# A diffusion block with a mixture of experts: gate/up of both experts of the first pair in turn, and router, heads, modulation steps, overflow branch and last pair rearranged

## The chip, the cores and the metric

The program runs on one core of one Trainium2 chip. The metric is the device time of one execution in microseconds (us). The names of the engines are those of the profile: PE is the matrix engine, PEld its weight loads, DVE the vector engine, ACT the scalar engine, POOL the general-purpose engine, SP the engine that issues the DMA transfers.

## The reference

256 latent tokens and 256 context tokens, 2048 wide, pass one block. Cut to what is computed:

```python
mod_x = jnp.split(jax.nn.silu(c) @ w_ada + b_ada, 6, axis=-1)          # 2048 x 12288
mod_c = jnp.split(jax.nn.silu(c_ctx)[None] @ w_ada + b_ada, 6, axis=-1)
qr, kr, vr, gr, cq, ckv, kpe = split_projection(modulate(x, mod_x[0], mod_x[1]) @ w_in)
qr_c, kr_c, vr_c, gr_c, cq_c, ckv_c, kpe_c = split_projection(modulate(ctx, mod_c[0], mod_c[1]) @ w_in)
...
o_ret = bidirectional_retention(qh, kh, to_heads(vr, 8), log_gamma, s_fwd, s_bwd)   # qh, kh: rope
ret = retention_output(o_ret, gr, ret_gn_w)
att = block_attention(q, concat(k_ctx, k_lat), concat(v_ctx, v_lat))    # 8 heads, low-rank q and kv
mix = jnp.concatenate([ret, from_heads(att)], -1) @ w_o
h = layer_norm(DEEPNORM_ALPHA * x + mod_x[2][:, None] * mix, ln1_w, ln1_b)
y = moe(modulate(h, mod_x[3], mod_x[4]))       # 4 groups of 8 experts, top group, top 2 in it
return layer_norm(DEEPNORM_ALPHA * h + mod_x[5][:, None] * y, ln2_w, ln2_b)
```

Each of the 32 experts has a gate and an up matrix of 2048 x 512 and a down matrix of 512 x 2048, in 4-byte numbers.

## The kernel before

A scheduler orders the instructions of each engine by the dependencies and the order of the source, so that the place in the source is only a wish, except in a block under `manual_schedule`, which keeps the source's order on the engines that it names. DMA loads are all issued by SP, in one order, each as soon as its buffer is free and SP has come to it.

**Input projection.** `w_in` is taken in six stages of 1, 1, 2, 4, 4 and 4 blocks of 128 rows (`STAGES`); within a stage ten blocks of columns pass, one load of 1 MB each in the stages of four (`win_chunks` gives their order, `ci` counts them). Each load is split into a high part (ACT, L273) and a low part (DVE, L274), and three matmuls for each 128x128 block multiply them (L594 to L596); a DVE addition collects the result (L603). Between the column blocks stand the pieces of the first two modulation vectors of the next stage: `piece(j, m)` loads 1 MB and issues matmuls with 32 rows of output (L526) for the shift (m=0) or the scale (m=1), into column groups 0, 1 or 2, 3 of the PE. All these loads turn over four buffers, `st`. `ada_steps` adds steps of the other four modulation vectors, 64 loads of 1 MB with two DVE multiply-adds each (L250); `ADA_V` says how many follow each column block, and at the end of the shift and scale for the experts `ada_finish` sums over the partitions with 16 one-column matmuls (L215).

**Heads.** In the last stage the rope on k (on POOL, L312 to L317) follows block ci=3; the rope on q (DVE), the decay tables and all eight retention heads (`ret_tables`, `ret_head`) follow ci=5, ahead of the last four blocks of columns. Latent attention and then the output projection `W_o` (L852 to L854, n = 0 to 3 for the column blocks) come after. With the first step of `W_o` four DVE reductions form the constants of the router (L810).

**Router.** After `W_o` the layer norm (L181, L182), the logits, the choice of the experts (L944 to L954) and the one-hot tables `oh` follow, mainly on DVE; PE waits for the choice at L957.

**Experts.** They go in 16 pairs (`pr`). A pair gathers its tokens with matmuls (`gather_two`, L1049, copied out by DVE L1058 and ACT L1055), multiplies them with gate and up (`gate_up`, L1071: expert e in four loads of 2 MB, c0 to c3), flips the hidden values, multiplies them with down (`down`, L1116, two loads d0 and d1; ACT L1122 and DVE L1123 split the result in a high and a low part) and puts it back (`scatter`, two matmuls L1130, DVE L1131 and L1132), which for most pairs stands in the next pair's `gate_up`. The loads (L1030) turn over six buffers, so that load n+6 waits until the matmuls of load n are done; the order of the loads is the list `order`. `overflow` after pair 5 is a branch for the case that more than 64 tokens chose one expert; it is not taken, but the branch is there. In the last pair (`final`) the two experts' down are interleaved, and statistics and the last norm follow.

## Time and profile before

| | us |
|---|---|
| median of three runs | 1685.78 |
| lowest and highest of them | 1684.48, 1687.98 |
| the profiled execution | 1686.18 |
| its span in the trace | 1684.4 |
| PE busy in it | 1521.6 |
| DVE busy in it | 919.9 |
| mean granted clock of the PE | 0.972 |

The span is the time from the first to the last record; what lies around it is 1.8 us here. A busy share alone says little: the stretches of the program have different limits, so that the rows further down are read stretch by stretch, for what each engine waits for.

### The profile page before, as it was taken

How to read it: one execution, taken by the hardware profiler on the slowest of the kernel's cores; microseconds unless marked ns; L12 is line 12 of the kernel's file. 1: busy time of each engine (PE TensorE's matmuls, PEld its weight loads, DVE VectorE, ACT ScalarE, POOL GpSimd, SP SyncE). 2: the span in 40 equal slices, each digit the busy share in tenths (PEclk: the TensorE clock that was granted, in tenths of full speed). 3: DMA queues.
4: the chain of work that ended last, by engine and by line, in shares of the span. 5: the costliest groups of instructions: out<-in, count | busy, mean ns of one | idle time of the engine just before them, and what ended most of it. 6: DMA issues, size and time to landing. Idle time of an engine off the chain costs nothing. (4 is left out here: it accounts for less than half of the span.)

```text
span 1684.4 us, 20454 instructions
## 1 busy us (share of the span) xinstructions
PE 1521.6 (90%) x8316; PEld 919.2 (55%) x8316; DVE 919.9 (55%) x1553; ACT 484.2 (29%) x913; POOL 105.9 (6%) x91
## 2 busy tenths in 40 slices
PE   5999999988889999699999988799989989899994
PEld 4667686877768767444543543444445345336432
DVE  6877584899698768824423532432342343234238
ACT  3323232324675534431320211121122013103112
POOL 1000000053513010000000000000000000000001
PEclk8999999998999999899999999999999999999997
DMA  8787777766554579579999999999999999999993
GB/s 326 272 326 283 294 309 286 276 245 225 184 192 153 199 270 360 225 301 426 426 427 427 426 427 425 370 428 427 427 427 427 427 426 427 426 426 427 421 425 136
DMA packets 54226, 579.28 MB, mean 344 GB/s; under 512 B 6320, under 2 KB 6768, under 8 KB 8816
## 3 DMA queue, kind: packets, MB, share of 16 engines
q1 hardware_dynamic: 54000, 577.90, 84.2%
q8 instruction: 67, 1.10, 0.3%
q14 instruction: 31, 0.25, 0.0%
q0 software_dynamic: 128, 0.03, 0.0%
HBM read 575.81 MB, written 2.10 MB: 343 GB/s over the span
## 5 line engine op out<-in xcount | busy, mean ns | idle before, releaser
L1071 PE MATMUL pA<-we,xg 128*64 128x512 f32 x2048 | 468.0, 602 | 12.8 <-DMA we<-in_wexp_dram 12.8
L1071 PEld LDWEIGHTS pA<-we,xg 128*64 128x64 f32 x2048 | 140.8, 138 | 281.2 <-issue 247.6
L1116 PE MATMUL pA<-we,hT 128*64 128x256 f32 x2048 | 232.7, 382 | 17.4 <-DMA we<-in_wexp_dram 16.1
L1123 DVE SCALAR_TENSOR_TENSOR D<-pA,gcol,D 64x256 fp32r<-64x256 f32 x256 | 123.5, 482 | 176.0 <-ACT D L1122 175.3
L273 ACT CAST whi<-st 128x1024 fp32r<-128x1024 f32 (+3 forms) x130 | 125.1, 965 | 282.5 <-PE pA L596 172.5
L1116 PEld LDWEIGHTS pA<-we,hT 128*64 128x64 f32 x2048 | 147.4, 137 | 92.2 <-ACT D L1122 8.7
L595 PE MATMUL pA<-wlo,xhi 128*128 128x512 f32 (+1 forms) x480 | 188.2, 392 | 10.5 <-DVE wlo L274 10.5
L594 PE MATMUL pA<-whi,xhi 128*128 128x512 f32 (+1 forms) x480 | 185.5, 394 | 3.3 <-ACT whi L273 3.1
L596 PE MATMUL pA<-whi,xlo 128*128 128x512 f32 (+1 forms) x480 | 185.8, 387 | 0.0
L250 DVE SCALAR_TENSOR_TENSOR ada_acc<-st,c,ada_acc 128x1024 f32<-128x1024 f32 x128 | 177.5, 1406 | 8.3 <-DMA st<-in_ada_dram 8.2
L274 DVE TENSOR_TENSOR wlo<-st,whi 128x1024 fp32r<-128x1024 f32 (+2 forms) x122 | 134.6, 1112 | 57.6 <-ACT whi L273 57.1
L1122 ACT ACTIVATE D<-pA,gcol 64x256 fp32r<-64x256 f32 x256 | 120.0, 469 | 156.7 <-PE pA L1116 87.5
L1074 ACT ACTIVATE hid<-pA 128x256 f32<-128x256 f32 x32 | 12.3, 383 | 493.5 <-PE pA L1071 493.5
L1075 DVE TENSOR_TENSOR hid<-pA,hid 128x256 f32<-128x256 f32 x32 | 13.5, 423 | 219.7 <-ACT hid L1074 219.7
L594 PEld LDWEIGHTS pA<-whi,xhi 128*128 128x128 f32 x480 | 90.5, 191 | 37.5 <-ACT whi L273 17.7
L595 PEld LDWEIGHTS pA<-wlo,xhi 128*128 128x128 f32 x480 | 91.9, 191 | 31.9 <-DVE wlo L274 14.5
L1058 DVE TENSOR_SCALAR xg<-pT,modt 128x256 f32<-128x256 f32 x64 | 34.8, 544 | 131.2 <-PE pA L1071 93.7
L1131 DVE TENSOR_TENSOR pA<-pA,ada_acc 128x512 f32<-128x512 f32 x128 | 83.5, 693 | 36.8 <-PE pA L1130 36.6
L596 PEld LDWEIGHTS pA<-whi,xlo 128*128 128x128 f32 x480 | 92.0, 192 | 16.3
L1049 PE MATMUL pT<-oh,nn 128*128 128x256 f32 x512 | 80.5, 303 | 9.1 <-DVEq L1136 5.8
L1049 PEld LDWEIGHTS pT<-oh,nn 128*128 128x128 f32 x512 | 68.3, 199 | 31.7 <-issue 20.5
L1132 DVE TENSOR_TENSOR h<-pA,h 128x512 f32<-128x512 f32 x128 | 82.6, 683 | 0.8
(353 smaller groups left out, 1578.6 us busy)
## 6 DMA issues: line engine op xcount, KB each, us to landing
we<-in_wexp_dram SPq DMA_DIRECT2D x190, 2048.0 KB, 21.8
st<-in_ada_dram SPq DMA_DIRECT2D x96, 1024.0 KB, 6.7
st<-in_win_dram SPq DMA_DIRECT2D x35, 1024.0 KB, 6.7
st<-in_wo_dram SPq DMA_DIRECT2D x16, 1024.0 KB, 4.9
we<-in_wexp_dram SPq DMA_DIRECT2D x4, 1024.0 KB, 17.4
st<-in_wuq_dram SPq DMA_DIRECT2D x3, 1024.0 KB, 4.8
xn<-in_x_dram SPq DMA_DIRECT2D x2, 1024.0 KB, 6.4
xn<-in_ctx_dram SPq DMA_DIRECT2D x2, 1024.0 KB, 17.0
```

What stands on the lines that cost most here:

```text
L250: V.scalar_tensor_tensor(accs[m][:, sl], w[:, sl], c2[:, k, 0:1], accs[m][:, sl], op0=OP.mult, op1=OP.add)
L273: A.copy(hi, src)
L274: (eng or V).tensor_tensor(lo, src, hi, op=OP.subtract)
L594: T.matmul(banks[t][:, :wd], xh[:, sl], hi[:, kk, :wd], start=fst, stop=False)
L595: T.matmul(banks[t][:, :wd], xh[:, sl], lo[:, kk, :wd], start=False, stop=False)
L596: T.matmul(banks[t][:, :wd], xl[:, sl], hi[:, kk, :wd], start=False, stop=lst)
L1049: T.matmul(p[:, 256 * j:256 * j + width], nnh[i % 2][:, i // 2, ks], oh[:, i // 2, :width], start=(i == 0), stop=(i == 3))
L1071: T.matmul(pg[64 * cg:64 * cg + 64], xg[:, k, c0:c0 + 64], c[:, kk, 512 * cg:512 * cg + 512], start=(k == 0), stop=(k == KB - 1))
L1116: T.matmul(pd[64 * cg:64 * cg + 64, :256], hT[:, f % 2, 64 * (f // 2):64 * (f // 2) + 64], c[:, f, 256 * cg:256 * cg + 256], start=(f == 0 ...
L1122: A.activation(hl[0][rows, sl], p, AF.Copy, scale=g)
L1123: V.scalar_tensor_tensor(hl[1][rows, sl], p, g, hl[0][rows, sl], op0=OP.mult, op1=OP.subtract)
L1131: V.tensor_tensor(p, p, mod5[:, sl], op=OP.mult)
```

## The change

- `piece(j)` takes both loads, shift and scale, and issues their matmuls in turn, so that four column groups of the PE follow each other; `GEMV_AT` places the pieces. The columns' order and `ADA_V` of the stages change; fewer `ada_steps` stand in the projection, more in the attention.
- `ada_finish` sums with four matmuls of 512 columns into the four column groups, an ACT copy and four transposes.
- The rope on k moves from POOL to DVE. Of the eight heads two follow each of ci=6 to 9, each head's tables two heads ahead.
- The four reductions of the router's constants are spread over four steps of `W_o`.
- Behind `W_o` the source's order is kept on DVE, ACT and PE. Only the norms that the first gathers need (c=0) and half of those of c=1 stand ahead of the choice of experts; the others follow it.
- In the first pair `gate_up` takes both experts, in turn for each gathered piece, and the first eight loads come in that order (`order[:8]`).
- The branch of `overflow` moves ahead of the downs of pair 5, whose gathers then run between the downs as in the other odd pairs.
- In the last pair D is kept whole (`new_D_whole`): no DVE subtraction, one matmul instead of two in `scatter`.

```diff
-ADA_V = [[0] * 10, [0] * 10, [0] * 5, [1] * 10, [1] * 10, [2] * 4 + [1] * 6]
+ADA_V = [[0] * 3, [1, 0, 0], [1, 1, 1, 0, 1], [1] * 7 + [0, 1, 1], [1] * 7 + [0, 1, 1], [1] * 10]
+
+GEMV_AT = (1, 3, 4, 5, 6)
...
+    elif si:
+        order = [0, 2, 1, 3, 6, 4, 7, 8, 5, 9]
...
-            for k in range(KB):
-                T.matmul(p[:, k:k + 1], acc[:, 128 * k:128 * k + 128], ones[:, 0:1], start=True, stop=True)
...
+            for g in range(4):
+                T.matmul(p[32 * g:32 * g + 32], ones[:, 0:32], acc[:, 512 * g:512 * g + 512], start=True, stop=True)
+            row = sa.tile([128, 2048], F32, name="st", tag="st")[:, :512]
+            A.copy(row, p)
+            p = bankT()
+            for j in range(4):
+                transpose(p[:, 128 * j:128 * j + 128], row[:, 128 * j:128 * j + 128])
...
-        def piece(j, m):
+        def piece(j):
...
+                c = [stream(dram2(a["ada01"], base + (m * nch + j) * 128 * per * w, 128, per * w), per * w)
+                     for m in range(2)]
                 for kk in range(per):
                     k = j * per + kk
-                    g = 2 * m + (k % 2)
-                    T.matmul(p[32 * g:32 * g + 32, :w], csil[:, k], c[:, kk * w:kk * w + w],
-                             start=(k < 2), stop=(k >= KB - 2))
+                    for m in range(2):
+                        g = 2 * m + (k % 2)
+                        T.matmul(p[32 * g:32 * g + 32, :w], csil[:, k], c[m][:, kk * w:kk * w + w],
+                                 start=(k < 2), stop=(k >= KB - 2))
...
-                            rope(pl["k"][:, t, 512 * j:512 * j + 512], t, "ck", "sk", 4, 64, R["rt"], G)
+                            rope(pl["k"][:, t, 512 * j:512 * j + 512], t, "ck", "sk", 4, 64, R["rt"])
...
-                    for h in range(H):
+                    for h in range(2):
                         ret_tables(h)
+                if ci > 5:
+                    for h in range(2 * ci - 12, 2 * ci - 10):
                         ret_head(h)
-                elif ci == LAT:
+                        if h < H - 2:
+                            ret_tables(h + 2)
+                if ci == LAT:
                     mla_latents()
...
+                if 1 <= 4 * n + k4 <= 4:
+                    router_const(4 * n + k4 - 1, rparts[4 * n + k4 - 1])
...
+        pinned = tc.manual_schedule(engines={V.engine, A.engine, T.engine})
+        pinned.__enter__()
...
+        norm_a(0, 0)
+        norm_a(1, 0)
+        V.reciprocal(hs[:, :, 1:2], hs[:, :, 1:2])
+        norm_b(0, 0)
+        norm_b(1, 0)
...
-    norms()
+    for c in range(1, 4):
+        for t in range(2):
+            if c > 1:
+                norm_a(t, c)
+            norm_b(t, c)
+            done, f = normed(t, c)
+            normed_lo(t, c, f)
...
+    order[:8] = [s * 6 + j for j in range(4) for s in range(2)]
...
-    def gate_up(xg, c0, src, before=None):
+    def gate_up(xg, experts, before=None):
...
+            for (c0, src), pg in zip(experts, pgs):
+                c = src(kc).rearrange("p (k n) -> p k n", k=2)
+                for kk in range(2):
+                    k = 2 * kc + kk
+                    for cg in range(2):
+                        T.matmul(pg[64 * cg:64 * cg + 64], xg[:, k, c0:c0 + 64], c[:, kk, 512 * cg:512 * cg + 512],
+                                 start=(k == 0), stop=(k == KB - 1))
...
+            if len(hl) > 1:
+                V.scalar_tensor_tensor(hl[1][rows, sl], p, g, hl[0][rows, sl], op0=OP.mult, op1=OP.subtract)
...
+            if len(hl) == 1:
+                T.matmul(p, sT[:K, t, :].bitcast(F32), hl[0][:K], start=True, stop=True)
...
+        pair = [(128 * pq + 64 * s, src[s]) for s in range(2)]
         if pr == 0:
-            router_weights()
-        hid1 = gate_up(xg, 128 * pq + 64, src[1], second)
+            hid0, hid1 = gate_up(xg, pair, first)
+            with tc.issue_after(done.ins):
+                router_weights()
+            for kc in range(8):
+                second(kc)
+        else:
+            hid0, = gate_up(xg, pair[:1], first)
+            hid1, = gate_up(xg, pair[1:], second)
         hT, sT, gcol = box["hT"], box["sT"], box["g"]
-        hl = new_D()
-        gather = pq and not final and pr != 5
+        if pr == 5:
+            overflow()
+        hl = new_D_whole() if final else new_D()
+        gather = pq and not final
```

The pieces of the modulation, on PE in the fourth stage. Before, the four matmuls of one piece stand between the triples of the projection:

```order
L594 MATMUL pA<-whi,xhi 128x512
L595 MATMUL pA<-wlo,xhi 128x512
L596 MATMUL pA<-whi,xlo 128x512
L526 MATMUL pG<-st,csil 32x512 x4
L594 MATMUL pA<-whi,xhi 128x512
L595 MATMUL pA<-wlo,xhi 128x512
```

The same place with the change (L603 to L605 are the projection's matmuls there, L535 the piece's):

```order
L603 MATMUL pA<-whi,xhi 128x512
L604 MATMUL pA<-wlo,xhi 128x512
L605 MATMUL pA<-whi,xlo 128x512
L535 MATMUL pG<-st,csil 32x512 x8
L603 MATMUL pA<-whi,xhi 128x512
L604 MATMUL pA<-wlo,xhi 128x512
```

Eight matmuls stand together where four stood; before, 13 such groups of four with 512 columns stood alone, and now none does, while in five of the 12 pieces with 512 columns one of the eight stands apart from the others.

The heads, on DVE in the last stage. Before, from the first head (`AM` are its scores, `stat` and `mv` its statistics) to the second:

```order
L396 TENSOR_TENSOR AM<-pA,Dt 128x256
L397 TENSOR_TENSOR AM<-pA,Dt 128x256
L250 SCALAR_TENSOR_TENSOR ada_acc<-st,c_71,ada_acc 128x1024 x2
L406 BN_STATS stat<-pA 128x6 x2
L407 BN_AGGR mv<-stat 128x2 x2
L396 TENSOR_TENSOR AM<-pA,Dt 128x256
```

With the change, from the first head to the second (L281 is the low part of a projection weight, L612 the projection's addition):

```order
L403 TENSOR_TENSOR AM<-pA,Dt 128x256
L404 TENSOR_TENSOR AM<-pA,Dt 128x256
L281 TENSOR_TENSOR wlo<-st,whi 128x1024
L612 TENSOR_TENSOR kvall<-pA,kvall 128x320 x4
L257 SCALAR_TENSOR_TENSOR ada_acc<-st,c_71,ada_acc 128x1024
L281 TENSOR_TENSOR wlo<-st,whi 128x1024
L413 BN_STATS stat<-pA 128x6 x2
L414 BN_AGGR mv<-stat 128x2
L257 SCALAR_TENSOR_TENSOR ada_acc<-st,c_71,ada_acc 128x1024
L414 BN_AGGR mv<-stat 128x2
L403 TENSOR_TENSOR AM<-pA,Dt 128x256
```

The column blocks that stood behind all eight heads now stand between them, with their splits and additions, and fewer halves of modulation steps do.

The first pair, on PE with the change, from the first `gate_up` on; between the rows shown are only gathers (`pA_5655` is the first expert's result with its loads c0 to c3 in `we_5642`, `we_5646`, `we_5650` and `we_5672`, `pA_5656` the second's in `we_5644`, `we_5648`, `we_5652` and `we_5708`):

```order
L1132 MATMUL pA_5655<-we_5642,xg_5654 64x512 x8
...
L1132 MATMUL pA_5655<-we_5646,xg_5654 64x512 x8
...
L1132 MATMUL pA_5655<-we_5650,xg_5654 64x512 x8
...
L1132 MATMUL pA_5656<-we_5644,xg_5654 64x512 x8
L1132 MATMUL pA_5656<-we_5648,xg_5654 64x512 x8
L1132 MATMUL pA_5656<-we_5652,xg_5654 64x512 x8
...
L1132 MATMUL pA_5655<-we_5672,xg_5654 64x512 x4
L1132 MATMUL pA_5656<-we_5708,xg_5654 64x512 x4
```

And the loads on SP with the change, from the first of the first pair on (`we_5672` takes the buffer of `we_5642`, `we_5708` that of `we_5644`, `we_5750` that of `we_5648`, `we_5714` that of `we_5646`):

```order
L1090 DMA we_5642<-in_wexp_dram 128x4096 [waits DMAHW5_49]
L1090 DMA we_5644<-in_wexp_dram 128x4096
L1090 DMA we_5646<-in_wexp_dram 128x4096 [waits DMAHW7_49]
L1090 DMA we_5648<-in_wexp_dram 128x4096 [waits DMAHW3_49,DMAHW2_49,DMAHW4_49,DMAHW1_49,DVE_49]
L1090 DMA we_5650<-in_wexp_dram 128x4096
L1090 DMA we_5652<-in_wexp_dram 128x4096
L1090 DMA we_5672<-in_wexp_dram 128x4096 [waits DMAHW5_49,PE_49]
L1090 DMA we_5708<-in_wexp_dram 128x4096 [waits DMAHW7_49,PE_49]
L1090 DMA we_5750<-in_wexp_dram 128x4096 [waits DMAHW1_49,PE_49]
L1090 DMA we_5714<-in_wexp_dram 128x4096 [waits DMAHW6_49,PE_49]
```

The second expert's pieces do not stand where the source has them: the first expert's first three go ahead, and c0 of the second stands behind c2 of the first, with six gathers between them. Before, the four pieces of the first expert came first and their loads stood first in the list.

## Rows read from the trace of the kernel before

**Rows 1.** Windows: start:end and length; busy PE, PEld, DVE, ACT, POOL; clock; DMA.

```profile
60.00:340.00 280.00, 278.69 (x1347) 199.53 (x1347) 199.04 (x255) 80.62 (x118) 2.30 (x2) 1.00 0.76 293
340.00:400.00 60.00, 54.17 (x221) 43.09 (x220) 56.46 (x75) 17.56 (x26) 30.34 (x28) 0.94 0.66 241
400.00:500.00 100.00, 83.50 (x451) 68.50 (x449) 84.95 (x176) 66.78 (x154) 39.47 (x32) 0.93 0.54 191
500.00:580.00 80.00, 75.19 (x443) 64.53 (x442) 67.92 (x120) 45.28 (x92) 15.23 (x6) 0.98 0.45 167
697.00:717.00 20.00, 6.18 (x29) 5.07 (x26) 18.26 (x75) 10.99 (x22) 0.00 (x0) 0.58 0.37 159
717.00:745.00 28.00, 28.00 (x144) 12.92 (x143) 8.52 (x22) 12.98 (x19) 0.00 (x0) 0.99 0.71 253
745.00:1060.00 315.00, 289.73 (x1720) 139.60 (x1718) 113.60 (x219) 61.59 (x133) 0.00 (x0) 0.99 1.01 426
1060.00:1100.00 40.00, 32.08 (x158) 17.46 (x158) 15.81 (x27) 5.89 (x12) 0.00 (x0) 0.91 0.91 368
```

**Rows 2.** The page's DMA issues: count, KB each, median us to landing.

```profile
we<-in_wexp_dram SPq DMA_DIRECT2D x190, 2048.0 KB, 21.8
```

**Rows 3.** Timeline of PE around two groups of pieces, from 118 and from 252 us.

```profile
118.66 1.94 PE L526 MATMUL pG<-st,csil 128*32 128x512 f32 x16
...
252.72 1.91 PE L526 MATMUL pG<-st,csil 128*32 128x512 f32 x8
```

**Rows 4.** Timeline of PE from 254 us: the sum of one modulation vector.

```profile
254.56 3.73 PE L215 MATMUL pT<-ones,ada_acc 128*128 128x1 f32 x32
```

**Rows 5.** One line on DVE, 120 to 320 and 361 to 379 us, ns min/median/max.

```profile
L250 DVE SCALAR_TENSOR_TENSOR ada_acc<-st,c,ada_acc x36: 1276/1279/1285, 123.7 to 311.2; 128x1024 f32<-128x1024 f32 x36
...
L250 DVE SCALAR_TENSOR_TENSOR ada_acc<-st,c,ada_acc x4: 1814/1818/1840, 361.7 to 372.0; 128x1024 f32<-128x1024 f32 x4
```

**Rows 6.** Groups of DVE instructions, 380 to 402 us: one of six rope operations.

```profile
L312 DVE TENSOR_TENSOR rp<-lq,rot 128x256 f32<-128x256 f32 x1 | 0.4, 417 | 0.0
```

**Rows 7.** Waits of 595 to 607 us: us in total, times, longest.

```profile
PE pA L853 <- DVE wlo L274: 4.1, 1, 4.1
```

**Rows 8.** Timeline of DVE from 592 us.

```profile
596.49 2.69 DVE L810 TENSOR_REDUCE rc<-st 128x40 f32<-128x640 f32 x2 [1.77 <-POOL st L806]
```

**Rows 9.** Timeline of PE from 690 us: end of `W_o` to the first pair.

```profile
690.68 0.40 PE L854 MATMUL pA<-whi,mix 128*128 128x512 f32 x1
...
712.03 0.60 PE L957 MATMUL pA<-sel,ct 128*128 128x32 f32 x2 [12.60 <-DVE w L992]
...
717.55 3.65 PE L1071 MATMUL pA<-we,xg 128*64 128x512 f32 x16
```

**Rows 10.** Groups of DVE instructions, 697 to 712 us, the largest.

```profile
L182 DVE SCALAR_TENSOR_TENSOR h<-h,hs,D 128x512 f32<-128x512 f32 x8 | 6.0, 748 | 0.0
```

**Rows 11.** Timeline of PE from 717 us, the first pair.

```profile
721.13 2.06 PE L1049 MATMUL pT<-oh,nn 128*128 128x256 f32 x15
...
724.81 3.65 PE L1071 MATMUL pA<-we,xg 128*64 128x512 f32 x14
...
733.27 1.94 PE L1071 MATMUL pA<-we,xg 128*64 128x512 f32 x8
...
738.59 5.37 PE L1071 MATMUL pA<-we,xg 128*64 128x512 f32 x24
```

**Rows 12.** The tile of the expert loads, 715 to 760 us.

```profile
DMA to landing us min/median/max: 7.6/11.2/15.3
```

**Rows 13.** Waits of 1060 to 1100 us: us in total, times, longest.

```profile
PE pT L1049 <- DVEq L1136: 5.8, 1, 5.8
```

**Rows 14.** Timeline of DVE from 1645 us, the last pair.

```profile
1649.10 0.70 DVE L1131 TENSOR_TENSOR pA<-pA,ada_acc 128x512 f32<-128x512 f32 x1
...
1661.39 0.49 DVE L1123 SCALAR_TENSOR_TENSOR D<-pA,gcol,D 64x256 fp32r<-64x256 f32 x1
...
1668.05 0.64 DVE L1181 BATCH_NORM_STATS2 st<-h 128x6 f32<-128x512 f32 x1
```

167 lines of the change are left out of this document (89 added, 78 removed).

## The prediction

> **What bounds the kernel now.** I read the busy shares first, in windows rather than over the span, because the limits differ [rows 1]. From 60 to 340 us PE is busy in 278.69 of 280 us while DMA stands at 0.76: every microsecond of PE time taken out there shortens the stretch. From 340 to 500 us neither PE (137.7 of 160) nor DVE (141.4) is full, and the clock is granted at 0.93 to 0.94: the two wait for each other. From 697 to 717 us PE has work for 6.18 of 20 us and DVE for 18.26: the choice of the experts is a DVE chain. From 745 us on the DMA share is 1.01 at 426 GB/s; the list of loads [rows 2] says what is moved, 190 loads of 2.097 MB and four halves, 402.7 MB, which take 943 us at that rate. So the end is the time at which the stream of expert weights runs full, plus 943 us, plus its holes, plus what DVE does behind its last byte. Work ahead of the stream counts fully if it moves its start.
>
> The sum is made against the profiled execution, 1686.18 us (span 1684.4 and 1.8 around it). It lies 0.4 above the median of the three runs, so the result is read against either. A change under 0.2%, 3.4 us, can't be told from none.
>
> **The pieces of the modulation: -13.** Eight records (four matmuls of two records) of a piece alone occupy PE for 1.91 us, sixteen records of two pieces mixed for 1.94 us [rows 3]: four column groups cost what two cost. The order shows 13 groups of four alone before and none after; each saves 1.91 - 1.94/2 = 0.94 us, together 12.2, and the pieces of 256 columns, half as wide, by my estimate about 1 us more. Nothing is taken for 128 columns, since the first 60 us also wait for transfers. Ends: -8, if the single matmul that stands apart in five pieces costs a round of its own and the pair of loads a wait; -18, if the narrow pieces halve too.
>
> **The sum of a modulation vector: -3.** 32 records, 3.73 us [rows 4], are replaced by four wide matmuls (0.97 by rows 3) and four short transposes, under 1 us. That saves 2 us in the full stretch; the second one lies among the heads, where PE waits anyway, for which I take 1. Ends -4 and -2.
>
> **Heads and last stage: -7.** The order shows the splits and additions of the last column blocks now between the heads. From 400 to 500 us PE has work for 83.50 us of 100 [rows 1]. If PE were as full as from 340 to 400, 54.17 of 60, the 83.5 would take 93 us: -7, my value. Ends: -17 with PE always busy, still above zero by DVE's 84.95; and +2, if the longer queue on DVE between two heads eats the overlap. The rope on k goes to DVE: 24 operations of 0.417 us [rows 6], 8 us of DVE work with the overlaps of its neighbours. Against that stands what POOL's rope does to DVE: the same step takes 1.82 us beside it and 1.28 without [rows 5], and 19 us of such company at that ratio cost about 6 us. The order shows six halves fewer of such steps by the heads' end, 6 x 1.28 = 8 us. All in all DVE has no more to do than before.
>
> The Trainium skill, "SBUF — State Buffer", section "SBUF: two separate sides", says that VectorE and GpSimd share one pair of ports as an exclusive lock, the loser blocking for the whole instruction. By that rule alone all 20 us of POOL's rope would block any DVE step of two SBUF operands, and the move would gain more than 6. The trace agrees only in part: in rows 5 the step is stretched by 0.54 us, not by the length of a POOL operation.
>
> **Attention: +2.** Four of the six halves come back there: 5 us of DVE work in a stretch where DVE has 12 us free and PE 5 [rows 1]. Ends 0 and +5.
>
> **Constants of the router: -4.** PE waits 4.1 us in one piece [rows 7] for a split queued behind the reductions, of which two take 2.69 us [rows 8]. Spread out, each stands alone among the splits of a step of `W_o`, in a stretch where DVE has time. Ends -5 and -1.
>
> **Router: -3.** From the last matmul of `W_o`, 690.68, to the first `gate_up`, 717.55, pass 26.9 us, 12.6 of them one wait of PE [rows 9]. Between 697 and 712 us the second halves of the norm alone (L182, eight of 0.75 us) take 6.0 us of DVE [rows 10]; with the change two of them and four first halves precede the choice, so that six second halves, 4.5 us, leave the chain, and with the four first halves at the same price 7 us. But the chain has hops to ACT and PE that the norms filled, and the norms of c=1 to 3 come back as a demand of the gathers. I take less than half. Ends -7 and 0.
>
> **First pair: +6.** This goes against the words of the change. Before, the first expert's pieces end near 721.2 [rows 9] and 728.5, 735.2 and 741 us [rows 11] (start and length of the last group of each; of the group from 738.59 a third), and each end frees a buffer. A load into an idle queue lands 7.6 us later at best [rows 12], so loads 7 to 10 land near 729, 736, 743 and 749, and then one every 4.9 us. With the change load 8 needs the buffer of the second expert's c0, and the order on PE puts that piece behind the first expert's c2, with SP unable to pass it. Counted from the first `gate_up`: c0 ends at +3.7, c2 between +15.4 (two times 2.2 us of gathers and 3.65 of matmuls) and +17.7 (the pace of before), say +16.5; six gathers and c0 of the second expert bring +21. Load 8 lands at +28.6 instead of +18.6. Behind it buffers are free in time, so load 10 lands at +38.4; before, it was 749.5 - 717.55 = +32. The stream is 6 us later relative to the first `gate_up`. PE has work all the while and shows no wait. Ends: -6 (a rival below) and +9.
>
> **Branch: -1.** From 1060 to 1100 us 368 GB/s instead of 426 [rows 1] lose 5.5 us of stream. SP still drains its queues at the branch; only PE's wait of 5.8 us [rows 13] and what it delays go. Ends -5 and +1.
>
> **Last pair: -4.** Behind 1649.10 DVE is the limit until the last statistics at 1668.05 [rows 14]; of its work nine subtractions (the last at 1661.39) fall away, 9 x 0.49 = 4.4 us. The single matmul on whole numbers may be longer than the two that it replaces, which the trace doesn't show; the 0.69 us of DVE between two scatters covers some of it. Ends -5 and -1.
>
> Sum: -13 - 3 - 7 + 2 - 4 - 3 + 6 - 1 - 4 = -27, so 1659 us.
>
> **Rivals.**
> - *The first pair is no loss*: both experts' pieces follow each gather as the source says, and buffers come free in twos. Loads 7 to 12 would then land at +12, +17, +22, +27, +32 and +37 instead of +12 to +42, 3 to 6 us earlier than before. Time 1659 - 11 = 1648. Against it: the order, which is what runs. 0.10.
> - *The heads fill PE wholly*, and the clock rises to 1.00: -17 instead of -7, 1649. For it: the blocks' matmuls need nothing of the heads; against it: DVE is the second limit at 85 us. 0.15.
> - *The heads wait behind the projection*, the other side: each head's chain crosses DVE twice, and if each of the eight waits once more behind a split (1.1 us) and a step of two halves (2.6), that is 30 us: 1659 + 7 + 30 = 1696, slower. It decides from about 4 us a head. For it: DVE works in order and the order shows those operations just there; against it: before, steps stood in the same places. 0.06.
> - *Nothing arrives*: the pairs of loads leave PE waiting one transfer of 1 MB (2.46 us at 426 GB/s) at each of the 12 wide pieces, 29 us, and the sum is back at 1688. For it: four buffers, two of them now taken by one piece; against it: DMA has a quarter of its time free there. 0.06.
>
> **How the numbers follow.** The forecast holds 0.63. Its own range takes the distances of the ends as independent: the root of the sum of their squares (5, 1, 9, 3, 3, 3, 3, 2 and 3 above; 5, 1, 10, 2, 1, 4, 4 and 1 below, the first pair's lower end being a rival) is 12 to 13 us to either side, 1646 to 1672. The two faster rivals lie at its lower edge, the two slower ones (0.12) outside; 1643 to 1674 holds 8 in 10. Faster than 1682 needs -3.4, which all cases but the last two give, less some of the spread: faster 0.87, same 0.05, slower 0.08.
>
> **What would show it.** Groups of eight piece matmuls (sixteen records) near 1.94 us; the stretch to the end of the fourth stage shorter by 10 or more; no 4 us wait of PE in the first steps of `W_o`; the first `gate_up` 23 to 25 us behind the last matmul of `W_o`; load 8 of the experts landing 27 to 30 us behind it, with a hole of 8 us or more in the stream ahead of it; a hole of about 4 us at the branch; no DVE subtraction in the last pair, and its end 4 us closer to the last landing. I am wrong if PE shows waits for `st` at the pieces, if heads wait for DVE longer than before, or if the stream has no hole at load 8.

## The result, and the profile after

The changed kernel takes 1662.17 us (median of four runs, 1660.17 to 1663.05), against 1685.64 of the kernel before in the runs beside them: a ratio of 0.9857, with a 95% interval of 0.9840 to 0.9874. The profiled execution took 1662.81 us, its span in the trace is 1661.0, its mean granted clock 0.970. The forecast of 1659 is 3.2 us off the median, under the 3.4 that can be told from nothing; its terms were less exact than their sum.

The two traces are compared at the same points of the program. A part's gain is what its stretch became shorter; the gains add up to the 23.4 us by which the profiled executions differ.

| point | before | after | gain of the part | forecast of the part |
|---|---|---|---|---|
| end of the fifth stage (360th high-by-low matmul, L596 and L605) | 338.26 | 330.41 | 7.9 | 15: pieces 13, their sum 3, less 1 of it for the heads |
| first matmul of `W_o` | 582.87 | 565.88 | 9.1 | 6: heads 7, sum 1, attention -2 |
| last matmul of `W_o` | 690.68 | 675.74 | -2.1 | 4 |
| first `gate_up` | 717.55 | 697.29 | 5.3 | 3 |
| load 24 of the experts lands | 818.96 | 797.84 | 0.9 | -6 |
| last load lands | 1653.60 | 1631.82 | 0.7 | 1 |
| end | 1684.40 | 1661.04 | 1.6 | 4 |

Windows of the kernel after, with the columns of [rows 1]:

```profile
60.00:340.00 280.00, 274.75 (x1360) 200.25 (x1360) 200.92 (x260) 83.02 (x122) 2.30 (x2) 0.99 0.76 295
400.00:500.00 100.00, 84.12 (x440) 66.87 (x440) 85.60 (x166) 73.43 (x165) 38.26 (x29) 0.91 0.49 181
...
100.00:120.00 20.00, 16.57 (x89) 10.01 (x86) 10.56 (x16) 5.77 (x12) 0.00 (x0) 0.94 0.92 351
120.00:145.00 25.00, 25.00 (x112) 20.76 (x112) 20.80 (x29) 8.46 (x14) 0.00 (x0) 0.91 0.75 278
...
676.00:697.00 21.00, 12.78 (x59) 8.08 (x58) 17.95 (x74) 8.79 (x15) 0.00 (x0) 0.86 0.65 275
720.00:1000.00 280.00, 266.47 (x1554) 127.42 (x1550) 107.97 (x212) 60.38 (x123) 0.00 (x0) 0.99 1.01 426
```

PE, full in the first stretch before [rows 1], now stands idle for 5.25 us of it (280 - 274.75), and most of that in one place: between 100 and 120 us PE works for 16.57 of 20 us while the DMA share is 0.92. Behind the first pair DMA is again the limit, at the same 426 GB/s. Timeline of PE (start, length, operation, what it waited for) at two pieces and the sum of a modulation vector:

```profile
108.54 4.54 PE L535 MATMUL pG<-st,csil 128*32 128x512 f32 x32
113.80 1.05 PE L544 MATMUL pG<-ct,row 128*128 128x4 f32 x8 [0.72 <-ACT row L541]
254.34 1.92 PE L535 MATMUL pG<-st,csil 128*32 128x512 f32 x16
256.09 1.04 PE L219 MATMUL pT<-ada_acc,ones 128*32 128x512 f32 x8
```

Sixteen records take 1.92 us where eight took 1.91 [rows 3]. The sum of a modulation vector takes 1.04 and, with its transposes (0.60), 1.64 instead of 3.73 us [rows 4]. PE's busy time of all piece matmuls, by their width, with the run two_groups from below beside it:

| columns (window of the trace, us) | forecast gain | before | after | two_groups |
|---|---|---|---|---|
| 128 (0 to 55) | 0 | 10.08 | 6.83 | 9.79 |
| 256 (55 to 82) | 1 | 9.68 | 6.74 | 8.84 |
| 512 (85 to 310) | 12.2 | 39.33 | 29.18 | 29.07 |

That is 16.3 us less PE work, and 2.1 less for the sum, but the end of the fifth stage comes only 7.9 us earlier: PE is busy for 305.5 us up to there instead of 319.3, since its other matmuls take longer, and idle for 24.9 instead of 19.0. By stages (60th, 120th, 240th and 360th high-by-low matmul) 3.3 us are won up to the end of the second, 5.3 lost in the third, 3.7 won in the fourth and 6.2 in the fifth.

The loss in the third lies at its seam with the fourth. At 108.54 two pieces stand together, whose four loads land one behind the other (at 100.9, 105.1, 108.6 and 111.1) and hold all four buffers. The pieces end at 113.1; before, the last one ended at about 108.9. SP could issue the next weights of the projection only at 110.51, when the first of the two pieces was done; they landed at 117.9, and PE, which until then had only the short matmuls for the next stage's input, went on with the projection at 119.58. The third stage's remaining blocks follow at a granted clock of 0.91 from 120 to 145 us, where the whole stretch before stood at 1.00 [rows 1].

The last stage up to the heads (360th to 440th high-by-low matmul), the columns as in [rows 1], first before and then after:

```profile
338.30:402.90 64.60, 58.77 (x242) 46.91 (x242) 60.84 (x86) 19.35 (x28) 30.34 (x28) 0.95 0.67 240
```

```profile
330.40:386.30 55.90, 54.97 (x243) 44.87 (x242) 53.77 (x106) 19.26 (x28) 5.79 (x4) 1.00 0.69 262
```

Here lie 8.7 of the 9.1 us that the heads' part of the table gained. Before, PE waited 5.8 us for splits of DVE in this stretch; now it waits 0.9, is nearly full, and its clock is granted at 1.00 instead of 0.95. DVE does 12 halves of modulation steps here instead of 17. From the 440th matmul to the first of `W_o` pass 179.6 us instead of 180.0, with 46 halves instead of 42.

In `W_o`, DVE and PE of the kernel after:

```profile
576.33 1.43 DVE L827 TENSOR_REDUCE rc<-st 128x40 f32<-128x640 f32 x1
...
579.54 1.40 DVE L827 TENSOR_REDUCE rc<-st 128x40 f32<-128x640 f32 x1 [1.78 <-POOL st L821]
580.85 1.74 DVE L281 TENSOR_TENSOR wlo<-st,whi 128x1024 fp32r<-128x1024 f32 x1
```

```profile
582.64 0.79 PE L876 MATMUL pA<-wlo,mix 128*128 128x512 f32 x1 [3.12 <-DVE wlo L281]
```

The picture of [rows 7] and [rows 8] is still there, only smaller. The scheduler put two of the four reductions back to back; the second waits 1.78 us on DVE for a product of POOL (L821), the split that PE needs stands behind it, and PE waits 3.12 us (4.1 before). The granted clock fell around that wait. Windows of 10 us in the kernel after and, for the same work, in the run constants_later below:

```profile
575.90:585.90 10.00, 6.88 (x24) 5.11 (x23) 8.22 (x7) 2.10 (x2) 5.33 (x7) 0.79 0.42 156
```

```profile
578.90:588.90 10.00, 9.01 (x39) 6.77 (x37) 9.28 (x7) 3.15 (x3) 8.10 (x7) 1.00 0.80 303
```

It fell to 0.79 in the window of the wait and stood at 0.87 for 10 us more; in the kernel before the same two windows show 0.93 and 0.90. With the wait split up it stays at 1.00. The shorter wait and the lower clock nearly cancel: the first 144 matmuls of `W_o` take 44.0 us instead of 43.6. The other 1.6 us of the 2.1 are lost later, at a granted clock of 1.00: from 622.8 to 650.1 us, 27.3 us, where 25.8 sufficed before (639.4 to 665.2); the router's sums (L857, L858) take 2.6 us of PE in there instead of 2.0, and PE idles 1.0 instead of 0.3. One execution says little here: in the seven other kernels below that leave `W_o` and the steps ahead of it as they are, it takes 108.1 to 110.1 us, against 109.9 here and 107.8 before.

From the end of `W_o` to the first pair, PE and ACT of the kernel after:

```profile
690.54 0.38 PE L1008 MATMUL pT<-sel,ct 128*128 128x32 f32 x2 [3.76 <-DVE sel L1003]
693.60 3.75 PE L1109 MATMUL pT<-oh,nn 128*128 128x256 f32 x16 [2.01 <-DVE oh L1020]
697.29 3.89 PE L1132 MATMUL pA<-we,xg 128*64 128x512 f32 x16
703.38 3.65 PE L1132 MATMUL pA<-we,xg 128*64 128x512 f32 x16
711.04 3.65 PE L1132 MATMUL pA<-we,xg 128*64 128x512 f32 x16 [0.45 <-DVE xg L1118]
716.55 10.52 PE L1132 MATMUL pA<-we,xg 128*64 128x512 f32 x48
728.76 7.09 PE L1132 MATMUL pA<-we,xg 128*64 128x512 f32 x32
```

```profile
715.91 2.04 ACT L239 COPY ada_acc<-pA 128x512 f32<-128x512 f32 x4
```

The router's chain is shorter: 21.6 us from the last `W_o` to the first `gate_up` instead of 26.9 [rows 9], with 18.2 us of DVE work in it instead of 25.1. The group of 48 records at 716.55 is the second expert's c0 to c2; it starts just as ACT copies the sums of the last modulation vector out of the PSUM bank that it takes. That could be why the order put c0 so late; copies_early below tests it. It did not delay load 8, though: SP issued it at 707.08, as the first expert's c1 ended (703.38 and 3.65), and it landed 18.3 us behind the first `gate_up`. The note on the loads in the section on the change names wrong buffers. `we_5708` (load 8) takes that of `we_5646`, with whose queue, DMAHW7, its own row there shows its wait; `we_5750` (load 9), issued at 714.73 as the first expert's c2 ended, takes that of `we_5650`; `we_5714` (load 10), issued at 720.24 as the second expert's c0 ended, takes that of `we_5644`. Loads 9, 10 and 12 landed at +25.0, +30.5 and +40.9; before, loads 8, 9, 10 and 12 at +18.7, +25.3, +32.7 and +42.5.

The last pair, DVE and PE of the kernel after:

```profile
1632.30 0.70 DVE L1204 TENSOR_TENSOR pA<-pA,ada_acc 128x512 f32<-128x512 f32 x1 [1.58 <-PE pA L1200]
```

```profile
1631.14 1.98 PE L1200 MATMUL pA<-D,sT 128*128 128x512 f32 x4
```

No subtraction is left on DVE (in [rows 14] it was the limit), but two scatters on whole numbers take 1.98 us, and DVE waits 1.58 for them, twice. From the last landing to the end pass 29.2 us instead of 30.8.

### The profile page after: what moved, and what is told of

The parts are those of the page before. It is cut to its first block, busy times and chain, and to the rows that moved or that the text cites. A ratio compares the mean times of both kernels' runs of the same rounds, so it can differ in the third digit from the quotient of the medians.

```text
span 1661.0 us, 20372 instructions
## 1 busy us (share of the span) xinstructions
PE 1512.3 (91%) x8276; PEld 906.1 (55%) x8276; DVE 912.8 (55%) x1560; ACT 486.7 (29%) x917; POOL 82.4 (5%) x67
## 5 line engine op out<-in xcount | busy, mean ns | idle before, releaser
L1185 PE MATMUL pA<-we,hT 128*64 128x256 f32 x2048 | 235.5, 384 | 18.6 <-DMA we<-in_wexp_dram 10.7
L1193 DVE SCALAR_TENSOR_TENSOR D<-pA,gcol,D 64x256 fp32r<-64x256 f32 x240 | 115.8, 483 | 175.8 <-ACT D L1191 175.1
L603 PE MATMUL pA<-whi,xhi 128*128 128x512 f32 (+1 forms) x480 | 183.0, 395 | 4.5 <-ACT whi L280 4.4
L605 PE MATMUL pA<-whi,xlo 128*128 128x512 f32 (+1 forms) x480 | 185.3, 386 | 0.0
L257 DVE SCALAR_TENSOR_TENSOR ada_acc<-st,c,ada_acc 128x1024 f32<-128x1024 f32 x128 | 172.6, 1365 | 6.1 <-DMA st<-in_ada_dram 6.1
L1191 ACT ACTIVATE D<-pA,gcol 64x256 fp32r<-64x256 f32 (+1 forms) x256 | 120.2, 470 | 161.7 <-PE pA L1185 100.4
L281 DVE TENSOR_TENSOR wlo<-st,whi 128x1024 fp32r<-128x1024 f32 (+2 forms) x122 | 134.5, 1111 | 45.7 <-ACT whi L280 45.4
L603 PEld LDWEIGHTS pA<-whi,xhi 128*128 128x128 f32 x480 | 90.0, 191 | 35.6 <-ACT whi L280 15.3
L605 PEld LDWEIGHTS pA<-whi,xlo 128*128 128x128 f32 x480 | 92.0, 192 | 16.6 <-DVE xlo L566 0.2
```

Of the source, the lines that this page charges most:

```text
L257: V.scalar_tensor_tensor(accs[m][:, sl], w[:, sl], c2[:, k, 0:1], accs[m][:, sl], op0=OP.mult, op1=OP.add)
L281: (eng or V).tensor_tensor(lo, src, hi, op=OP.subtract)
L603: T.matmul(banks[t][:, :wd], xh[:, sl], hi[:, kk, :wd], start=fst, stop=False)
L605: T.matmul(banks[t][:, :wd], xl[:, sl], hi[:, kk, :wd], start=False, stop=lst)
L1185: T.matmul(pd[64 * cg:64 * cg + 64, :256], hT[:, f % 2, 64 * (f // 2):64 * (f // 2) + 64], c[:, f, 256 * cg:256 * cg + 256], start=(f == 0 ...
L1191: A.activation(hl[0][rows, sl], p, AF.Copy, scale=g)
```

## The experiments

The theory when the runs were planned: the heads' stretch gained because steps left it and the heads spread; the pieces' gain was partly given back at the seam between third and fourth stage; the pair's new order was worth about nothing. The rivals stand with each run. Each run changes the kernel after; its median is to be read against 1662.17, its ratio is against the kernel before.

**two_groups: the two loads of a piece one after the other.**

```diff
-                for kk in range(per):
-                    k = j * per + kk
-                    for m in range(2):
+                for m in range(2):
+                    for kk in range(per):
+                        k = j * per + kk
                         g = 2 * m + (k % 2)
```

> The changed kernel with the matmuls of a piece's shift ahead of those of its scale, so that again only two column groups of the PE stand side by side; loads, places and everything else as in the change. If the side-by-side column groups are what the merged pieces bring, each of the 12 wide pieces takes 0.94 us more and the kernel is 9 to 13 us slower than the changed one, near 1673 us. If transfers or the clock set the pace there, as the waits near 110 us in the changed kernel's trace could mean, it is within 4 us of 1662.

1673.79 us, ratio 0.9937 (0.9920 to 0.9954). The size came out as expected of the loss of four groups, for another reason. PE of this run:

```profile
302.35 1.94 PE L535 MATMUL pG<-st,csil 128*32 128x512 f32 x16
```

The sixteen records still take 1.94 us, and from the 240th to the 360th high-by-low matmul pass 92.54 us against 92.65. The loss is elsewhere: 4.7 us by the 60th, where the narrow pieces lie, and some 6 in the last stage (360th to 440th: 61.8 instead of 55.9), where the scheduler laid DVE's work otherwise. For the wide pieces, then, the run does not test the term: the order within a piece is not needed there, only that the eight matmuls stand together. For the narrow pieces, in which 8 or 16 matmuls to two groups now stand ahead of the other two groups, it does: they take 18.6 us of PE instead of 13.6 (table above), nearly as long as before the change (19.8). So there the side-by-side column groups are the cause.

**no_steps_stage3: the four steps of the third stage back in the last one.**

```diff
-ADA_V = [..., [1, 1, 1, 0, 1], ..., [1] * 10]
+ADA_V = [..., [0] * 5, ..., [2] * 4 + [1] * 6]
```

> The changed kernel with the four modulation steps of the third stage put into the last stage instead. Theory: their 4 MB of loads stand ahead of the last pieces' four loads and make the seam between the third and fourth stage late (the 32 records of the last two pieces end at 113.1 us, 4 us later than before the change, and the clock falls); then the seam comes 4 us sooner and the kernel takes about 1659 us, less what the last stage pays for four more steps (up to 5 us). Rival: the two pieces' four loads in a row fill all four buffers whatever stands ahead; then the seam stays within 1 us and the time is 1662 or more.

1669.07 us, 0.9902 (0.9885 to 0.9918). The seam is where it was (120th matmul 144.5 instead of 144.9), so the steps of the third stage do not cause it; the four loads of the two pieces, which hold all buffers, stay as the cause that the trace shows, and no run takes them apart. The first `W_o` comes at 574.26 instead of 565.88: four steps in the last stage cost 8.4 us. Windows and waits of PE (us in total, times, longest) of this run and, for the same work, of the kernel after:

```profile
329.00:455.00 126.00, 112.05 (x559) 93.23 (x559) 115.77 (x233) 66.26 (x142) 37.32 (x30) 0.96 0.58 219
...
PE pA L409 <- DVE AM L403: 6.3, 5, 2.0
PE pA L604 <- DVE wlo L281: 5.4, 2, 4.9
```

```profile
330.00:450.00 120.00, 112.18 (x563) 92.73 (x563) 107.88 (x228) 65.57 (x141) 35.83 (x30) 0.97 0.55 205
...
PE pA L409 <- DVE AM L403: 2.7, 3, 2.0
PE pA L604 <- DVE wlo L281: 0.9, 1, 0.9
```

PE has the same 112 us of work; DVE has 8 more and PE waits for it. With these four steps DVE is the limit of this stage; without them PE is nearly full, as the rows above show.

**heads_together: all eight heads behind ci=5, as before.**

```diff
-                    for h in range(2):
+                    for h in range(H):
                         ret_tables(h)
-                if ci > 5:
-                    for h in range(2 * ci - 12, 2 * ci - 10):
                         ret_head(h)
-                        if h < H - 2:
-                            ret_tables(h + 2)
```

> The changed kernel with all eight heads again behind the column block ci=5. If spreading the heads between the last column blocks is what shortened the last stage, as the prediction had it at 7 us, the kernel takes 1668 to 1671 us and output projection starts 7 to 9 us later. Rival: the fewer steps on DVE and the rope taken off POOL did it; then it is within 2 us of 1662.

1675.47 us, 0.9941 (0.9924 to 0.9958). The heads end at 432.2 instead of 461.1, but only 64 halves of steps are done by then instead of 76, and the rest comes back later: the first matmul of `W_o` comes at 571.30, 5.4 later, the last at 688.63, 12.9 later. Waits of PE in `W_o`:

```profile
PE pA L872 <- DVE wlo L281: 5.6, 3, 3.2
PE pT L173 <- DVE h L893: 4.9, 3, 3.7
```

Spreading the heads is worth 5.4 us at their place and 7.5 more behind it.

**rope_pool: the rope on k back on POOL.**

```diff
-                            rope(pl["k"][...], t, "ck", "sk", 4, 64, R["rt"])
+                            rope(pl["k"][...], t, "ck", "sk", 4, 64, R["rt"], G)
```

> The changed kernel with the rope on k on POOL again. By the prediction DVE gains the 8 us of the operations and loses some 6 as its own steps stretch beside POOL (1.82 instead of 1.28 us each): within 2 us of 1662. Rival, the port pair as an exclusive lock for whole instructions: up to 19 us of POOL work block DVE where it is the limit; 1668 us or more.

1669.30 us, 0.9902 (0.9886 to 0.9918): 7 us more, the first `W_o` 7.2 later (573.11). Timelines of POOL and DVE of this run from 353 us:

```profile
353.63 0.75 POOL L320 TENSOR_TENSOR rp1p<-lk,rot 128x256 f32<-128x256 f32 x1
354.33 1.73 POOL L322 TENSOR_TENSOR lk<-lk,rot 128x256 f32<-128x256 f32 x1
356.02 0.73 POOL L321 TENSOR_TENSOR lk<-lk,rot 128x256 f32<-128x256 f32 x1
```

```profile
353.63 1.83 DVE L257 SCALAR_TENSOR_TENSOR ada_acc<-st,c,ada_acc 128x1024 f32<-128x1024 f32 x1
355.38 0.71 DVE L346 TENSOR_SCALAR r_z<-r_z 128x16 f32<-128x16 f32 x1
356.61 0.18 DVE L345 TENSOR_TENSOR r_z<-r_z,r_w 128x16 f32<-128x16 f32 x1
```

Like operations of POOL take 0.73 or 1.73 us, and a DVE operation that starts behind one takes 0.53 to 0.55 more, be it 1.28 or 0.18 us long by itself: a fixed delay, not a shared rate. Where DVE starts first, as the split at 357.40 does, it takes its usual 1.21 us and POOL's operation 1.80. DVE's additions that read PSUM (L612, 0.68 us at 356.01) are not delayed. So the two engines take turns by instruction. The Trainium skill, "SBUF — State Buffer", section "SBUF: two separate sides", says of a DVE operation with two SBUF inputs (or in a two-port mode) and a POOL operation that reads SBUF that whichever starts first has the shared ports for its whole instruction and the other fully blocks. The turns agree with it; why the delay is 0.53 and not the 0.73 of a POOL operation, the rows do not tell.

The turns alone do not explain the 7 us. From 340 to 372 us 17 DVE operations are delayed, by 9.1 us in sum against the shortest like operations of the kernel after; as operations of DVE the rope's 24 take 8 to 10 (0.335 to 0.417 each). The two nearly balance. The rest goes with the order that the scheduler found without the rope on DVE: up to the 440th high-by-low matmul it puts 16 halves of steps instead of 12, from 357.40 to 368.97 no split stands on DVE, and PE is busy for 4.89 of 10 us from 360 to 370. How much is blocking and how much order, no run tells.

**steps_earlier: nearly all steps of the last stage moved to the fourth and fifth.**

```diff
-ADA_V = [..., [1] * 7 + [0, 1, 1], [1] * 7 + [0, 1, 1], [1] * 10]
+ADA_V = [..., [2, 1, 2, 1, 1, 1, 1, 1, 2, 1], [2, 1, 2, 1, 1, 1, 1, 1, 2, 1], [0] * 6 + [1, 0, 1, 0]]
```

> The changed kernel with eight of the ten modulation steps of the last stage moved to the fourth and fifth stage. Four steps more in the last stage cost 8.4 us up to the start of the output projection, so DVE is a limit there, while it is busy 71% of the time from 60 to 340 us. Theory: the eight steps are free in the stages ahead and bring 2.1 us each where they are taken out, less as PE becomes full: 8 to 17 us, 1645 to 1654. Rival: their 8 MB meet the pieces' loads and make PE wait for weights in the fourth and fifth stage (DMA share 0.73 to 0.84 there); then half or more is given back, 1656 or later.

1667.23 us, 0.9889 (0.9869 to 0.9910): 5 more. The 240th to the 300th matmul take 59.9 us instead of 50.4. Window and waits of PE there:

```profile
236.00:297.00 61.00, 54.91 (x238) 38.70 (x237) 44.34 (x45) 11.47 (x11) 0.62 (x2) 0.92 0.83 332
...
PE pA L604 <- DVE wlo L281: 3.0, 3, 1.8
PE pA L603 <- ACT whi L280: 2.9, 1, 2.9
```

DVE is busy in 44 of 61 us only; PE waits for splits that came late, the DMA share is 0.83 and the clock 0.92. The full stages have DVE time to give, but not at any rate of loads. And the last stage gave nothing back. The same stretch as above, 360th to 440th, of this run:

```profile
338.80:394.20 55.40, 54.75 (x243) 44.99 (x242) 42.94 (x96) 19.36 (x28) 7.04 (x4) 1.00 0.36 127
```

DVE has 10.8 us less work there than in the kernel after, but the stretch is only 0.5 shorter, because PE was nearly full already; up to the first `W_o` pass 235.9 us instead of 235.5. The theory of 2.1 us for each step taken out failed: four steps more cost 8.4, five fewer bring nothing.

**pair_in_turn_undone: the first pair as before, first expert and then second.**

```diff
-    order[:8] = [s * 6 + j for j in range(4) for s in range(2)]
...
-            hid0, hid1 = gate_up(xg, pair, first)
+            hid0, = gate_up(xg, pair[:1], first)
...
-            for kc in range(8):
-                second(kc)
+            hid1, = gate_up(xg, pair[1:], second)
```

> The changed kernel with the first pair as before: one gate/up after the other and their loads in the old order. By the prediction the change of the first pair costs 6 us, so that without it the kernel takes 1656 us and load 8 of the experts lands near 18.6 us behind the first gate/up instead of 28.6. By the changed kernel's trace, where load 8 lands 18.3 us behind it and load 12 at 40.9 instead of 42.4, the change of the first pair is worth 0 to 1.5 us of gain: 1662 to 1664 us.

1667.41 us, 0.9895 (0.9878 to 0.9912). Both theories missed: load 12 lands 44.9 us behind the first `gate_up` instead of 40.9, and the time is 5.2 us longer. Taken alone, the pair's new order gains 4 to 5 us. The trace had hidden that, because with the rest of the change the old order is dearer than it was before, +44.9 against +42.5: PE now waits 2.3 us in the pair for norms and gathered copies, and for none before. That fits the norms that now follow the choice.

**pair_pinned: the first pair's pieces in turn on PE, in the order that the source wishes.**

```diff
-            hid0, hid1 = gate_up(xg, pair, first)
+            with tc.manual_schedule(engines={T.engine}):
+                first(0)
+                first(1)
+                for kc in range(0, 8, 2):
+                    half(0, kc)
+                    half(0, kc + 1)
+                    if kc < 6:
+                        first(kc + 2)
+                    half(1, kc)
+                    if kc < 6:
+                        first(kc + 3)
+                    half(1, kc + 1)
```

> The changed kernel with the order on PE held by hand in the first pair: c0 of both experts, then c1 of both and so on, with the gathers of the next piece between, as the source reads. The buffers then come free in twos from the first gathered piece on. By the arithmetic of the rival in the prediction load 12 lands 36 us behind the first gate/up instead of 40.9, and the kernel takes about 1657 us. Rival: the norms and copies that the gathers wait for set the pace, not the order of the pieces; then load 12 stays within 1.5 us of 40.9 and the time near 1662.

1676.17 us, 0.9944 (0.9925 to 0.9964): 14 more. PE of this run, and ACT:

```profile
715.88 3.68 PE L1294 MATMUL pA<-we,xg 128*64 128x512 f32 x8 [13.82 <-ACT ada_acc L239]
```

```profile
715.25 2.04 ACT L239 COPY ada_acc<-pA 128x512 f32<-128x512 f32 x4
```

The whole loss is one wait: the second expert's bank is held by sums that ACT copies only at 715 us. The scheduler's order had worked round it.

**copies_early: these copies ahead of the choice of experts.**

```diff
     fs = [normed(t, 0)[1] for t in range(2)]
+    for f in mod5_copies:
+        f()
...
     nnfs.close()
-    for f in mod5_copies:
-        f()
     pinned.__exit__(None, None, None)
```

> The changed kernel with the four ACT copies of the last modulation vector's sums taken ahead of the choice of the experts instead of behind all the norms. Their PSUM banks are what the second expert of the first pair waits for: in the changed kernel the copies run at 715.9 to 717.9 us and the second expert's first piece starts at 716.6. Theory: with the banks free at 690 us the pieces of the two experts alternate as the source reads, load 12 lands 36 to 37 us behind the first gate/up instead of 40.9, and the kernel takes 1657 to 1658 us. Rival: the copies delay the norms of the first gathers, or the gathers set the pace; then load 12 stays within 1.5 us of 40.9 and the time near 1662.

1664.02 us, 0.9874 (0.9858 to 0.9890): no gain. With the bank free, the order follows the source by itself, and so finely that the matmuls of both experts alternate within a piece (PE of this run):

```profile
697.60 7.92 PE L1132 MATMUL pA<-we,xg 128*64 128x512 f32 x32
705.45 2.06 PE L1109 MATMUL pT<-oh,nn 128*128 128x256 f32 x15
```

The first buffer comes free only at +6.2 us and the second at +7.9; load 7 lands at +13.9 instead of +11.6, load 12 at +41.0, as before the edit.

**pair_pinned_free: both, copies early and the order pinned.**

> The same early copies, and the order on PE held by hand in the first pair as in the run before: c0 of the first expert, c0 of the second with the gathers between, and so on. If the 13.8 us that PE waited there were for the bank alone, they are gone, load 12 lands near +36 and the kernel takes 1657 us; if the order by hand is itself at fault (copies of the gathered piece late), PE waits at each piece and the time is 1662 or more.

1661.06 us, 0.9858 (0.9841 to 0.9874). The wait of 13.8 us is gone and load 12 lands at +39.4, 1.5 us earlier than in the kernel after; the median is 1.1 lower, which the spread of the runs does not tell from nothing. PE of this run:

```profile
694.95 4.46 PE L1294 MATMUL pA<-we,xg 128*64 128x512 f32 x16
699.34 1.21 PE L1109 MATMUL pT<-oh,nn 128*128 128x256 f32 x8
700.48 1.94 PE L1294 MATMUL pA<-we,xg 128*64 128x512 f32 x8
```

PE waits for nothing here and sets the pace itself: eight pieces of 3.65 us and the gathers of 1.2 between them.

**constants_later: each of the router's four reductions bound behind a split, one step of `W_o` later.**

```diff
-                if 1 <= 4 * n + k4 <= 4:
-                    router_const(4 * n + k4 - 1, rparts[4 * n + k4 - 1])
+                if 2 <= 4 * n + k4 <= 5:
+                    with tc.issue_after(split_at["last"].ins):
+                        router_const(4 * n + k4 - 2, rparts[4 * n + k4 - 2])
```

> The changed kernel with each of the four reductions of the router's constants held behind the second split of the third to sixth step of the output projection. In the changed kernel the second reduction waits 1.8 us on DVE for POOL's product, with a split queued behind it, and PE waits 3.1 us. Theory: with the products long done that wait goes, and the clock stays up; 3 to 4 us less, about 1658.5. Rival: the stall moves to another split, since DVE is 75% busy there; within 1 us of 1662.

1660.44 us (1656.01 to 1662.71), 0.9845 (0.9822 to 0.9868). Waits of PE in `W_o`, of this run and of the kernel after:

```profile
PE pA L878 <- DVE wlo L281: 2.1, 5, 0.8
```

```profile
PE pA L876 <- DVE wlo L281: 3.9, 3, 3.1
```

Now the reductions stand alone, and `W_o` takes 106.2 us instead of 109.9; its first 144 matmuls take 40.4 instead of 44.0, and 43.6 in the kernel before. In this execution it began 2.8 us later, so that the end, 1660.94, is that of the kernel after, and the medians do not tell the two apart: the trace shows the mechanism, the time does not show the gain.

**split_last_pair: D of the last pair in two parts again.**

```diff
-        hl = new_D_whole() if final else new_D()
+        hl = new_D()
```

> The changed kernel with the last pair's result split in a high and a low part again, as before. The prediction gave whole numbers a gain of 4 us: 1666 us. The two traces have 30.8 us before and 29.2 after from the last landing to the end, since the single matmuls are longer (1.98 us for two of them instead of 1.20 for two pairs) and DVE waits for them: by that 1663.7 us.

1665.34 us (1663.22 to 1666.32), 0.9885 (0.9866 to 0.9903), whose interval overlaps that of the kernel after. PE of this run:

```profile
1634.51 1.21 PE L1203 MATMUL pA<-D,sT 128*128 128x512 f32 x4
...
1638.24 1.98 PE L1203 MATMUL pA<-D,sT 128*128 128x512 f32 x4 [2.52 <-ACT D L1191]
```

Both at a granted clock of 1.00, the scatters in pairs take 1.21 us at 1634.51 and whole ones 1.98; but the next ones in pairs wait 2.52 for ACT's part of D and then take 1.98 themselves, at a granted clock of 0.60. From the last landing to the end pass 30.2 us against 29.2. So the whole D gains 1 us by the trace and 3 by the medians: at most a small gain, its size open.

**pair_constants: pair_pinned_free and constants_later together.** These two touched separate waits and neither lost, so they were joined.

> The early copies and the order by hand in the first pair together with the later reductions of the router's constants: the version with all that the runs showed to help. If the output projection's 3.7 us, which came with a start of it 2.8 us later, are real, and the first pair gives 4 to 5: 1653 to 1656 us. If the projection's gain was only moved from the wait ahead of it, 1657.

1658.27 us (five runs, 1655.96 to 1658.70), 0.9832 (0.9818 to 0.9847): the fastest version. `W_o` takes 105.9 us and load 12 lands at +38.8. It clearly beats the kernel before; against the kernel after it is 3.9 us ahead, with intervals that overlap a little (0.9840 to 0.9847).

## Why the prediction came out as it did

The time came within 3.2 us because errors of both signs cancelled, which is luck: the pieces and their sum brought 7.1 us less than forecast up to the end of the fifth stage and the constants 6.1 less, while the first pair came out 6.9 better and the heads 3.1. The mechanism of the largest term, the pieces, held; its size did not.

- *Pieces, -13 and -3 for their sum*: the step "four column groups cost what two cost" held, 1.92 us. PE's saving was even larger than forecast, 16.3 + 2.1 us, because the narrow pieces, taken at 1 and at nothing, gave 2.9 and 3.3; the wide ones gave 10.2 of 12.2. But only 7.9 arrived, so the term was mis-sized by what the seam between third and fourth stage and the lower clock behind it gave back. Of the rival "the pairs of loads leave PE waiting one transfer" something came true at one place, where two pieces held all four buffers. The 3.3 us won by the end of the second stage were not in the forecast.
- *Heads, -7 (with attention and the sum, 6)*: 9.1 measured, but by another step and at another place. "If PE were as full as from 340 to 400" did not come from 400 to 500 us, where PE is busy for 84.12 of 100 us, as before. It came ahead of the heads, where PE is now busy for 54.97 of 55.9 us instead of 58.77 of 64.6, at a clock of 1.00: that part of the rival "The heads fill PE wholly" was right. What shortened the stretch is that DVE no longer holds PE up: with four steps more 8.4 us are lost (no_steps_stage3), with the rope on POOL 7 (rope_pool), with the heads together 5.4 at their place (heads_together). These prices don't add up to the 9.1, since each is taken with the others in place, and they end where PE is full (steps_earlier). The rival of the heads behind the projection did not come.
- *Rope*: "the trace agrees only in part" failed. A short DVE operation is delayed by the same 0.53 us as a long one, and POOL's operation by 1.0: both block in turn. The 0.54 that I held against the rule is the delay of one such turn. The sum "no more to do than before" held: 9.1 us of delays against 8 to 10 of operations. That the move is still worth 7 us it does not tell.
- *Attention, +2*: not measured by itself; with four halves more, the stretch behind the 440th matmul is 0.4 us shorter.
- *Constants, -4*: the step "each stands alone among the splits" failed; two stood together, and the stretch grew by 2.1, 0.4 of it up to the 144th matmul. constants_later, where each stands alone, takes 40.4 us for that first part instead of the 43.6 before: the mechanism was right, the order was not what I took it for. What the router's sums lose behind it was not in the forecast.
- *Router, -3*: 5.3, nearer to its end of 7. The trace shows the step given, 6.9 us less of DVE work in the chain; no run takes it alone.
- *First pair, +6*: the step "load 8 needs the buffer of the second expert's c0" failed. The buffers had been handed out in the order in which they come free, and the loads' own rows of waits said so. With the change undone the pair is 4 to 5 us slower; even the rival "no loss" came short in mechanism, because the pieces of both experts in turn free the buffers hardly faster, load 12 at +41.0 (copies_early) and +39.4 (pair_pinned_free) instead of +37: PE sets the pace. The 749.5 us for load 10 before does not follow from its rows, which give 740.4 + 7.6 = 748.0; the trace has 750.2.
- *Branch, -1*: 0.7. The hole at the branch stands in both traces, as forecast: two loads land 9.0 us apart instead of 4.9.
- *Last pair, -4*: 1.6; mis-sized. The whole-number scatters cost 1.98 us instead of 1.21, the size that the text had left open.
- *The signs that it named*: the groups of 1.94 us, the hole at the branch and the missing subtractions came. The end of the fourth stage came only 1.7 us earlier, not 10; a wait of 3.1 us stayed in `W_o`; the first `gate_up` came 21.6 us behind the last `W_o`, sooner than the 23 to 25; load 8 landed at +18.3, 6.7 us behind load 7 as before, so the stream has no new hole, and by its own words the account of the first pair was wrong.
- *A sum*: 402.7 MB at 426 GB/s take 945 us, not 943; nothing is built on it.

## What to carry to other kernels

A saving of engine work is worth its full size only as long as the transfers keep up: where two loads must now be there at once, look for the place at which they hold all the buffers, so that the next load cannot go out. Which buffer a load takes is read from the semaphore that it waits on, not from its name or place; and an order that looks odd may be working round a bank that another engine frees late, so free the bank before pinning the order. Where two engines wait for each other, price an edit by the work that it takes off the fuller one, and only until the other engine is full: here four steps more cost 8.4 us and five fewer brought nothing. And compare traces between the same points of the program; in windows of equal time the gain of the heads' part did not show.

## What the runs showed of the hardware that was not expected

- Matmuls of 32 output columns overlap with those of other column groups also when the program order puts the same groups in between: with four matmuls to groups 0 and 1 and then four to 2 and 3, each 512 wide, the sixteen records still took 1.94 us (two_groups), where eight records of two groups alone take 1.91 [rows 3]. With 8 or 16 narrower matmuls to two groups ahead of the others most of that overlap is gone: 8.84 and 9.79 us of PE instead of 6.74 and 6.83.
- The delay between DVE and POOL does not depend on the size of the delayed operation: one of 128x16 took 0.71 instead of 0.18 us, one of 128x1024 1.83 instead of 1.28 (rope_pool).
- At a granted clock of 1.00 two matmuls of 128x512 on whole 4-byte numbers take 1.98 us of PE, the four that they replace 1.21.
